# A mixture-of-experts layer whose stored expert results are weighted before they leave the chip and added to the residual stream by indirect DMAs

## The chip, the cores and the metric

The program runs on one core of a Trainium2 chip, in one launch. The metric is the device time of an execution in microseconds. The engines that appear below are PE (TensorE: matmuls and transposes), DVE (VectorE), ACT (ScalarE), POOL (GpSimd, which also issues the indirect DMAs) and SP (which issues plain DMAs). Each runs its own queue of instructions in order; semaphores tie them together. Line numbers (L1252) are those of the kernel before, unless the changed kernel is named.

## The reference

Two layers over 256 latent and 256 context tokens of width 1024, four blocks of 128 tokens; layer 1 gives out the latent tokens alone, so its experts work on two blocks. What matters here is the second half of a layer and the begin of the next:

```python
        h = _ln(x) * (1 + sc2) + sh2
        x = _ln_affine(ALPHA * x + g2 * _hier_moe(h, w_rg[l], b_rg[l], w_re[l], b_re[l], w1[l], w3[l], w2[l]),
                       ln2_g[l], ln2_b[l])
        # and the same for the context with sh2c, sc2c, g2c
...
def _hier_moe(h, w_rg, b_rg, w_re, b_re, w1, w3, w2):
    # top-1 group of 4, top-2 of its 8 experts: combine[t, e] holds the two weights of token t
    for e in range(N_EXPERTS):
        hidden = jax.nn.silu(h @ w1[e]) * (h @ w3[e])
        out = out + combine[..., e:e + 1] * (hidden @ w2[e])
```

`sh2`, `sc2`, `g2` come from `silu(c) @ w_mod[l] + b_mod[l]`, one set for latent tokens and one for context tokens. The next layer begins with `_ln(x) * (1 + sc1) + sh1` and the projection `h @ w_in[l]`.

## The kernel before

Every tile of size lies in units of 8 KB per partition that `Mem` hands out. Weights are a list in the order of use (`stream`); `pump` issues as many loads from it as units and a cap (`cap`, set per place from HC and MC) allow, and `drop` frees a unit when its matmuls are done. Expert weights are loaded by indirect DMAs that POOL issues (L142), all other weights by SP (L161). The modulation `c @ w_mod` is cut into steps of one 1 MB load and four matmuls (L320); those of the next layer are `fillers`, put by `fill(n)` where TensorE would wait.

Layer 0's experts are worked off in passes (`todo`, from PLAN). A pass gathers its tokens by one-hot matmuls (L1191), computes both up projections (`up`, L1204), transposes the hidden rows (`mid`, L1238) and multiplies by `w2`. The last two passes (HOME = 2) weight their results and add them over a one-hot matmul on chip (`back` L1227, `down` L1262, `combine` L1284). The twelve passes before these ("away") write theirs unweighted to the DRAM buffer `ys`: `put` copies the two halves of a 128x1024 tile out of PSUM, one on ACT and one on DVE (L1252), and SP stores it (L1254). Afterwards each token needs two rows of `ys`, its two experts: `fetch` gathers them by indirect DMAs into `ACC` and `two` (L1482), and `fold` does the rest for a block: ACT scales the first row by its weight (L1489), DVE adds the second times its weight (L1491), multiplies by g2 (L1492) and adds to `X` (L1493). Blocks 0 and 1 are fetched during the last two passes, blocks 2 and 3 behind the loop `rest`.

`rest` is a hardware loop over token lists that did not fit the plan; it runs no round in the profiled execution, but all engines pass its entry and exit (L1501), and nothing is moved across it. Behind it come the last `combine`, the second DeepNorm (`deepnorm`, `moments`: sums on DVE L427, means L414/L415, squares on ACT L416, inverse root on POOL L419, L431/L433 on DVE), the LayerNorm of the next layer, its transposes (`turned`, L489, evicted by ACT L497 and DVE L494), and the projection `p_qa`, three matmuls per product of split operands (L457 to L459). Before, loads for layer 1 are taken from the stream during the last expert passes, as units come free. A scheduler lays out each engine's queue from the order written here and priorities; `tc.issue_after` gives it an order.

## Time and profile before

| | us |
|---|---|
| median of 3 runs | 1111.08 (1108.67 to 1111.8) |
| profiled execution | 1106.13 |
| its span | 1104.2 |
| TensorE busy | 994.6 (90%) |
| DVE, ACT, POOL busy | 511.2, 353.1, 302.0 |
| layer 0's expert passes, by TensorE | 342.95 to 597.2 |
| layer 1's first projection begins | 642.61 |

Rows of a timeline give start, duration and instruction, and in brackets how long the engine stood idle before it and what ended that (`<-DMA u<-ys,find` is the landing of a DMA from `ys`). Rows of a group give the busy time in total and the mean of one in ns. Windows give per stretch the busy time of each engine, the granted clock of TensorE as a share of 2.4 GHz, the share of time in which the DMA engines moved data, and the rate.

### The profile page before, as it was taken

The page shows a single profiled execution, that of the slowest core. Times are in us where ns is not written, and L with a number is a line of the kernel's source. Part 1 is how long each engine was busy: PE and PEld are TensorE (multiplying, and loading weights), DVE is VectorE, ACT ScalarE, POOL GpSimd, SP SyncE. Part 2 cuts the span into 40 slices and gives each one's busy share as a digit, 9 for nine tenths or more (in the row PEclk, how much of TensorE's full clock was granted, in tenths as well). Part 3 has the DMA queues.
Part 4 walks back from the last instruction along what each step waited for, and adds up shares of the span by engine and source line. Part 5 has one row for each costly group of instructions (what it writes and reads, how often), then busy time and mean ns, then how long its engine had stood idle before and what let it go on. Part 6 is the DMA issues. An engine that isn't in the chain of part 4 may idle for free. (4 is left out here: it accounts for less than half of the span.)

```text
span 1104.2 us, 14811 instructions
## 1 busy us (share of the span) xinstructions
PE 994.6 (90%) x5525; PEld 571.6 (52%) x5525; DVE 511.2 (46%) x1364; ACT 353.1 (32%) x712; POOL 302.0 (27%) x325
## 2 busy tenths in 40 slices
PE   4999999999999999999985479999998899999894
PEld 2788745457866454444332259844466554433231
DVE  5643357775577210100013887266666654242244
ACT  4533155563552111111112365144444222111111
POOL 2111133350001432343341222042300145344420
PEclk9999999999999999999998789999997899999997
DMA  9812157610269999999998653435425799999992
GB/s 374 321 64 88 48 191 278 218 44 34 107 259 390 399 423 422 363 414 421 423 421 352 249 202 112 173 137 193 150 78 230 306 387 423 421 421 421 420 421 90
DMA packets 46207, 300.54 MB, mean 272 GB/s; under 512 B 5394, under 2 KB 5778, under 8 KB 14388
## 3 DMA queue, kind: packets, MB, share of 16 engines
q0 software_dynamic: 25824, 177.81, 39.2%
q1 hardware_dynamic: 20308, 121.75, 29.4%
q8 instruction: 45, 0.74, 0.3%
q14 instruction: 30, 0.25, 0.1%
HBM read 292.19 MB, written 7.34 MB: 271 GB/s over the span
## 5 line engine op out<-in xcount | busy, mean ns | idle before, releaser
L142 POOL DMA_INDIRECT u<-in_w_exp,u x162 | 161.1, 994 | 307.4 <-PE psa L1204 95.9
L1204 PE MATMUL psa<-u,u 128*32 128x512 f32 (+2 forms) x1040 | 212.9, 596 | 8.1 <-DMA u<-in_w_exp,u 8.1
L458 PE MATMUL psa<-u,u 128*128 128x512 f32 (+3 forms) x400 | 140.0, 351 | 2.2 <-DVE u L452 2.2
L457 PE MATMUL psa<-u,u 128*128 128x512 f32 (+3 forms) x400 | 140.8, 356 | 0.9 <-ACT u L506 0.7
L459 PE MATMUL psa<-u,u 128*128 128x512 f32 (+3 forms) x400 | 139.1, 351 | 0.1
L1204 PEld LDWEIGHTS psa<-u,u 128*32 128x32 f32 (+2 forms) x1040 | 64.6, 126 | 132.5 <-issue 109.1
L1191 PEld LDWEIGHTS psc<-u,u 128*128 128x128 f32 x640 | 83.0, 197 | 33.2 <-issue 29.0
L1191 PE MATMUL psc<-u,u 128*128 128x256 f32 x640 | 93.7, 297 | 3.0 <-DVE u L1177 2.1
L889 POOL TENSOR_SCALAR u<-u,ri 128x512 f32<-128x512 f32 (+1 forms) x48 | 68.4, 1430 | 99.1 <-DVE ri L887 81.5
L1211 DVE TENSOR_TENSOR scr<-scr,psa 128x256 f32<-128x256 f32 x26 | 10.9, 421 | 163.4 <-ACT scr L1210 157.7
L458 PEld LDWEIGHTS psa<-u,u 128*128 128x128 f32 x400 | 76.1, 190 | 12.9 <-DVE u L452 4.3
L457 PEld LDWEIGHTS psa<-u,u 128*128 128x128 f32 x400 | 75.5, 190 | 12.2 <-ACT u L506 1.1
L459 PEld LDWEIGHTS psa<-u,u 128*128 128x128 f32 x400 | 75.4, 190 | 9.3 <-issue 0.9
L886 ACT ACTIVATE u<-psa,nm 128x512 f32<-128x512 f32 (+1 forms) x96 | 58.4, 615 | 54.7 <-DVE nm L884 49.8
L1262 PE MATMUL pse<-u,scr 128*64 128x512 f32 (+1 forms) x288 | 70.4, 599 | 0.8 <-DMA u<-in_w_exp,u 0.8
L452 DVE TENSOR_TENSOR u<-u,u 128x1024 fp32r<-128x1024 f32 (+4 forms) x38 | 56.1, 1486 | 19.5 <-ACT u L451 19.4
L1210 ACT ACTIVATE scr<-psa 128x256 f32<-128x256 f32 x26 | 10.0, 385 | 171.5 <-PE psa L1204 171.5
L1193 ACT ACTIVATE u<-psc 128x512 f32<-128x512 f32 x52 | 31.1, 597 | 101.5 <-PE psc L1191 58.9
L884 DVE TENSOR_REDUCE nm<-psa 128x1 f32<-128x512 f32 (+1 forms) x80 | 53.1, 683 | 13.1 <-PE psa L874 9.5
L419 POOL TENSOR_TENSOR lns<-lns,mhalf 128x1 f32<-128x1 f32 x22 | 14.2, 648 | 162.7 <-DVE lns L418 130.3
L1249 PE MATMUL pse<-u,scr 128*32 128x512 f32 (+2 forms) x232 | 57.3, 600 | 1.4 <-ACT scr L1239 1.4
L451 ACT ACTIVATE u<-u 128x1024 fp32r<-128x1024 f32 (+4 forms) x38 | 47.4, 1266 | 16.2 <-PE psa L458 3.5
(317 smaller groups left out, 1366.5 us busy)
## 6 DMA issues: line engine op xcount, KB each, us to landing
u<-in_w_mod SPq DMA_DIRECT2D x48, 1024.0 KB, 6.5
u<-in_w_exp SPq DMA_DIRECT2D x30, 1024.0 KB, 6.9
u<-in_w_out SPq DMA_DIRECT2D x8, 1024.0 KB, 4.8
ys<-u SPq DMA_DIRECT2D x12, 512.0 KB, 8.2
u<-in_w_in_b SPq DMA_DIRECT2D x10, 512.0 KB, 11.7
u<-in_w_in_v SPq DMA_DIRECT2D x4, 960.0 KB, 5.9
u<-in_w_in_qa SPq DMA_DIRECT2D x4, 768.0 KB, 11.7
u<-in_ln_rows SPq DMA_DIRECT2D x6, 512.0 KB, 7.1
```

What stands on the lines that cost most here:

```text
L142: G.indirect_dma_start(out=b.ap(UNIT), out_offset=None, in_=wexp_rows, in_offset=bass.IndirectOffsetOnAxis(ap=idx, axis=0), bounds_check=N ...
L452: V.tensor_tensor(l_[:, c], w[:, c], h[:, c].bitcast(F32), OP.subtract)
L457: PE.matmul(p, lhsT=a[0], rhs=b[0], start=first, stop=False)
L458: PE.matmul(p, lhsT=a[0], rhs=b[1], start=False, stop=False)
L459: PE.matmul(p, lhsT=a[1], rhs=b[0], start=False, stop=final)
L884: V.tensor_reduce(out=nm[:, s, 0:n], in_=pv, axis=AX.X, op=OP.max, negate=True)
L886: S.activation(P[:, i, :], pv[:, i, :], AF.Exp, bias=nm[:, s, i:i + 1], accum_out=su[:, s, i:i + 1])
L889: (G if s == 0 else V).tensor_scalar(P[:, i, :], P[:, i, :], ri[:, s, i:i + 1], None, op0=OP.mult)
L1191: PE.matmul(pv[:, j, :], lhsT=H[b][:, k * 128:(k + 1) * 128], rhs=OH[:, b, :], start=(b == 0 and i == 0), stop=(b == nb - 1 and i == 1))
L1204: PE.matmul(g[r, :], lhsT=XG[:, k, at * 128 + r.start:at * 128 + r.stop], rhs=W(t, k // 4).v(4, 512)[:, k % 4, :], start=(k == 0), stop=(k ...
L1249: PE.matmul(y[r, :], lhsT=hc[:, c * 128 + r.start:c * 128 + r.stop], rhs=W(t, 2).v(2, D)[:, c, f * 512:f * 512 + 512], start=(c == 0), sto ...
L1262: PE.matmul(y[r, :], lhsT=hc[:, c * 128 + r.start:c * 128 + r.stop], rhs=W(t, 2).v(2, D)[:, c, f * 512:f * 512 + 512], start=(c == 0), sto ...
```

## The change

The weights and g2 are put on an expert's result before it is stored. `shares` forms, per away pass, two weights for each of the 128 rows, one if the row belongs to a latent token and one if to a context token (the other is zero), by four small matmuls; `put` computes y·w0·g2 + y·w1·g2c by two scalar_tensor_tensor on DVE and an add on POOL per half. `X` is scaled by ALPHA during pass 2, and `fetch` adds the rows of `ys` into `X` by an indirect DMA with `compute_op=add`, eight of them; `fold` and its buffers go, `yo` has two buffers for three, g2's rows are made at pass 0. Layer 1's part of the stream is held back until behind `rest` (`upto`; the first modulation group excepted), `rows()` (the DeepNorm's gain and bias, L1465) is loaded there too, and freshly freed units are used first for a while (`newest`). Its order mixes modulation steps between projections; of four `fill` steps ahead of the projections two go behind the two `p_b`. MC falls from 11 to 10 units and HC changes.

```diff
-MC = (11, 15)
+MC = (10, 15)
...
-HC = (8, 7, 3, 5)
+HC = (10, 10, 3, 3, 5)
...
@@ pump
+            if key[1] > upto[0] and key[0:3] != ("mod", 1, 0):
+                return
...
@@ the stream of layer 1
-    for k in ("qa", "cq"):
-        for c in range(2):
-            stream_chunk(k, 1, c)
+    for c in range(2):
+        stream_chunk("qa", 1, c)
+    stream_mod(1, 1, 0, 2)
+    for c in range(2):
+        stream_chunk("cq", 1, c)
     for c in range(2):
         stream_b(1, c)
-    stream_mod(1, 1, 0, 4)
+        stream_mod(1, 1, c + 2, c + 3)
...
@@ layer, its begin in layer 1
             rest_of()
+            fill(2)
             for c in range(2):
                 presplit("qa", c)
             make_h()
-            fill(4)
...
+            pump(HC[4])
+            mem.newest = False
             together(*[before(b, xn) for b in range(2, 4)])
             p_qa()
             p_cq()
             for c in range(2):
-                p_b(c)
+                gate[:] = [p_b(c)]
+                fill(1)
+            gate.clear()
...
+        def shares(q, at, n, m, col):
+            OH = ohs[q % len(ohs)].v(nb, 128 * n)
+            e = 128 // m
+            ws = sm.tile([128, 2], F32, name="ws", bufs=2)
+            p = bank("a")
+            for b in range(nb):
+                o = b // 2 * 2 * e
+                PE.matmul(p[:, o:o + 2 * e], lhsT=OH[:, b, at * 128:at * 128 + 128], rhs=IW[:, b, :, col:col + e],
+                          start=(b % 2 == 0), stop=(b % 2 == 1))
+            for t, r in enumerate(slots(m)):
+                V.tensor_reduce(out=ws[r], in_=p[r, 0:4 * e].rearrange("p (s i e) -> p s e i", s=2, i=2)[:, :, t],
+                                axis=AX.X, op=OP.add)
+            return ws
...
@@ put
-                d = Y[:, f * 512:f * 512 + 512]
-                V.tensor_copy(d, y) if f else S.activation(d, y, AF.Copy)
+                fs = slice(f * 512, f * 512 + 512)
+                w = scratch()
+                V.scalar_tensor_tensor(w, y, ws[:, 0:1], BC["g2", 0][:, fs], op0=OP.mult, op1=OP.mult)
+                V.scalar_tensor_tensor(Y[:, fs], y, ws[:, 1:2], BC["g2", 1][:, fs], op0=OP.mult, op1=OP.mult)
+                G.tensor_tensor(Y[:, fs], Y[:, fs], w, OP.add)
...
@@ fetch
-            for b in blocks:
-                acc[b] = mem.get(D)
-                ACC[b] = acc[b].v(D)
-                two.append(mem.get(D))
-                for dst, j in ((ACC[b], 0), (two[b].v(D), 1)):
-                    G.indirect_dma_start(out=dst, out_offset=None, in_=ys[:, :],
+            for j in range(2):
+                for b in blocks:
+                    G.indirect_dma_start(out=X[b], out_offset=None, in_=ys[:, :],
                                          in_offset=bass.IndirectOffsetOnAxis(ap=find[:, b, j:j + 1], axis=0),
-                                         bounds_check=at_row, oob_is_err=False)
+                                         bounds_check=at_row, oob_is_err=False, compute_op=OP.add)
-        def fold(blocks):
-            for b in blocks:
-                S.activation(ACC[b], ACC[b], AF.Copy, scale=sc_[:, b, 2:3])
-            for b in blocks:
-                V.scalar_tensor_tensor(ACC[b], two[b].v(D), sc_[:, b, 3:4], ACC[b], op0=OP.mult, op1=OP.add)
-                V.tensor_tensor(ACC[b], ACC[b], BC["g2", b // 2], OP.mult)
-                V.tensor_tensor(X[b], X[b], ACC[b], OP.add)
-                two[b].free()
...
@@ the passes, and behind them
+            if i < away:
+                ws = shares(q, at_, n, m, col)
             hc = mid(hb)
...
-                put(i, hc, m, W, rel)
+                put(i, hc, ws, m, W, rel)
...
         rest(slot[held[0]], qe % 2)
...
-        pump()
+        if not last:
+            mem.newest = True
+            rows()
+            upto[0] = 1
+            pump(HC[2])
...
-            fold(range(2))
```

The scheduler's order shows three places. On TensorE, in the changed kernel, the end of the fifth pass: `shares` is L1257, `mid`'s transposes are L1268, the last up matmuls L1219.

```order
L1219 MATMUL psa<-u_3732,u_3032 128x512 x4
L1257 MATMUL psa<-u_3036,u_3035 128x2 x4
L1268 MATMUL psa<-ident,scr 128x128 x2
L1219 MATMUL psa<-u_3728,u_3032 128x512
L1279 MATMUL pse<-u_3752,scr 128x512 x4
```

The four matmuls are new there; in the order before, the transposes follow the up matmuls directly.

On POOL, behind the loop `rest`, in the kernel before: L1482 are the fetches, L308 the loads of b_mod, L419 the inverse roots.

```order
L1482 DMA u_4690<-ys,find 128x1024
L1482 DMA u_5038<-ys,find 128x1024
L1482 DMA u_4697<-ys,find 128x1024 [waits DVE_49]
L308 DMA u_99<-in_b_mod 4x512 x2
L306 MEMSET u_99 128x512
L308 DMA u_99<-in_b_mod 4x512 [waits Pool_49]
L308 DMA u_99<-in_b_mod 4x512
L419 TENSOR_TENSOR lns<-lns,mhalf 128x1 [waits DVE_49] x6
```

And in the changed kernel, the same place, where L1508 are the adding fetches into `X` of blocks 2 and 3 (`u_72`), L315 the loads of b_mod, L427 the inverse roots.

```order
L1508 DMA u_72<-ys,find 128x1024 x2
L315 DMA u_99<-in_b_mod 4x512
L1508 DMA u_72<-ys,find 128x1024 [waits DMASW4_49]
L1508 DMA u_72<-ys,find 128x1024 [waits DMASW5_49]
L315 DMA u_99<-in_b_mod 4x512
L313 MEMSET u_99 128x512
L315 DMA u_99<-in_b_mod 4x512 [waits Pool_49]
L315 DMA u_99<-in_b_mod 4x512
L427 TENSOR_TENSOR lns<-lns,mhalf 128x1 [waits DVE_49] x6
```

The second add of each block now waits on POOL for a DMA, ahead of the inverse roots; before, no fetch behind the loop waits for another.

On DVE, before the evictions of the transposes (L494), in the kernel before: L1491 to L1493 are the fold of blocks 2 and 3, L1293 the evictions of `combine`.

```order
L437 TENSOR_TENSOR lns<-lns 128x1
L1491 SCALAR_TENSOR_TENSOR u_4697<-u_4998,sc__2337,u_4697 128x1024
L1491 SCALAR_TENSOR_TENSOR u_4690<-u_5038,sc__2337,u_4690 128x1024
L1492 TENSOR_TENSOR u_4697<-u_4697,u_4597 128x1024
L1492 TENSOR_TENSOR u_4690<-u_4690,u_4597 128x1024
L1493 TENSOR_TENSOR u_72<-u_72,u_4697 128x1024
L1493 TENSOR_TENSOR u_72<-u_72,u_4690 128x1024
L1293 TENSOR_TENSOR u_4697<-psa,u_4597 128x512 x2
L1293 TENSOR_TENSOR u_4690<-psa,u_4597 128x512 x2
L494 TENSOR_SCALAR scr<-psc,modT_100 128x256 x2
```

And in the changed kernel, where L443 is the former L437, L458 splits qa's weights, L433 adds `combine`'s rows to `X` of block 2, and L500 is the former L494.

```order
L443 TENSOR_TENSOR lns<-lns 128x1 [waits Pool_49]
L458 TENSOR_TENSOR u_5308<-u_5163,u_5307 128x512 [waits DMAHW1_49]
L458 TENSOR_TENSOR u_5308<-u_5163,u_5307 128x512 x2
L433 SCALAR_TENSOR_TENSOR u_72,dns<-u_72,u_5168 128x1024 [waits DMASW7_49]
L500 TENSOR_SCALAR scr<-psc,modT_100 128x256 [waits Activation_49] x2
```

The fold is gone from between the second norm's statistics and the evictions, and a sum that waits for the second adding fetch of block 2 stands in its place.

## Rows read from the trace of the kernel before

**Rows 1.** The page, busy time, share of the span and instructions of TensorE

```profile
PE 994.6 (90%) x5525; PEld 571.6 (52%) x5525; DVE 511.2 (46%) x1364; ACT 353.1 (32%) x712; POOL 302.0 (27%) x325
```

**Rows 2.** Windows around the seam: engines' busy us, clock, DMA share, GB/s

```profile
342.95:597.20 254.25, 239.13 (x1241) 108.00 (x1240) 36.72 (x121) 37.96 (x72) 88.25 (x89) 1.00 1.00 408
597.20:604.20 7.00, 0.02 (x1) 0.00 (x0) 3.08 (x3) 1.90 (x3) 0.00 (x0) 0.77 0.60 238
604.20:622.00 17.80, 12.51 (x48) 7.38 (x48) 14.45 (x28) 8.09 (x13) 7.75 (x10) 0.88 0.90 326
622.00:642.60 20.60, 6.80 (x32) 3.03 (x33) 18.59 (x37) 7.81 (x11) 2.32 (x3) 0.52 0.38 119
```

**Rows 3.** TensorE's timeline behind the loop: start us, us, instruction [idle before]

```profile
612.91 1.06 PE L320 MATMUL pse<-u,csil 128*32 128x512 f32 x8
...
629.52 1.54 PE L489 MATMUL psc<-ident,u 128*128 128x128 f32 x6 [1.40 <-ACT u L438]
638.03 3.64 PE L320 MATMUL pse<-u,csil 128*32 128x512 f32 x16 [6.97 <-DMA u<-in_w_mod]
...
642.61 0.42 PE L457 MATMUL psa<-u,u 128*128 128x384 f32 x1
```

**Rows 4.** TensorE's waits in the passes: us in total, times, longest

```profile
PE psa L1204 <- DMA u<-in_w_exp,u: 7.0, 5, 2.7
PE psa L1238 <- DVE scr L1211: 5.9, 6, 1.0
```

**Rows 5.** TensorE's timeline at the end of the passes

```profile
585.61 3.65 PE L1204 MATMUL psa<-u,u 128*64 128x512 f32 x14 [2.70 <-DMA u<-in_w_exp,u]
...
593.58 3.65 PE L1262 MATMUL pse<-u,scr 128*64 128x512 f32 x12 [0.21 <-DMA u<-in_w_exp,u]
604.47 6.39 PE L1284 MATMUL psa<-u,u 128*128 128x512 f32 x20 [7.25 <-issue]
```

**Rows 6.** Groups of the passes: busy us, mean ns, idle before

```profile
L1252 DVE COPY u<-pse 128x512 f32<-128x512 f32 x12 | 8.3, 691 | 67.1 <-PE pse L1249 67.1
...
L1227 PE MATMUL psa<-u,u 128*128 128x4 f32 x8 | 1.2, 256 | 0.0
```

**Rows 7.** SP's DMA issues for layer 1, first and last of seven

```profile
566.32 0.33 SPq L161 DMA_DIRECT2D u<-in_w_in_qa  x1
...
589.35 0.37 SPq L161 DMA_DIRECT2D u<-in_w_in_b  x1
```

**Rows 8.** Groups of the whole span

```profile
L889 POOL TENSOR_SCALAR u<-u,ri 128x512 f32<-128x512 f32 x32 | 51.4, 1608 | 65.0 <-DVE ri L887 65.0
...
L1271 DVE SCALAR_TENSOR_TENSOR u<-pse,ws,u 128x512 fp32r<-128x512 f32 x4 | 3.0, 749 | 8.7 <-ACT u L1270 8.7
```

**Rows 9.** DMA issues: count, KB each, median us to landing

```profile
ys<-u SPq DMA_DIRECT2D x12, 512.0 KB, 8.2
...
u<-in_w_exp,u POOLq DMA_INDIRECT x162, 16.4
```

**Rows 10.** SP's waits from 560 to 645: us in total, times, longest

```profile
SPq L1501 <- DMA u<-ys,find: 13.1, 4, 6.1
```

**Rows 11.** DVE's timeline around the end of the loop

```profile
599.98 0.74 DVE L1271 SCALAR_TENSOR_TENSOR u<-pse,ws,u 128x512 fp32r<-128x512 f32 x1
...
628.04 2.48 DVE L1491 SCALAR_TENSOR_TENSOR u<-u,sc__2337,u 128x1024 f32<-128x1024 f32 x2
...
634.97 2.48 DVE L1293 TENSOR_TENSOR u<-psa,u 128x512 f32<-128x512 f32 x4
637.37 0.99 DVE L494 TENSOR_SCALAR scr<-psc,modT 128x256 f32<-128x256 f32 x2
```

**Rows 12.** ACT's timeline behind the loop

```profile
612.96 1.15 ACT L1489 ACTIVATE u<-u,sc__2337 128x1024 f32<-128x1024 f32 x1 [5.39 <-DMA u<-ys,find]
```

**Rows 13.** POOL's timeline behind the loop

```profile
604.87 1.55 POOL L1482 DMA_INDIRECT u<-ys,find  x1 [14.35 <-issue]
...
618.18 0.94 POOL L419 TENSOR_TENSOR lns<-lns,mhalf 128x1 f32<-128x1 f32 x1 [5.69 <-DVE lns L418]
```

More of the change, by code (lines that the diff above doesn't have):

```diff
@@ L1 @@
 import math
-from contextlib import ExitStack
+from contextlib import ExitStack, nullcontext
 import numpy as np
@@ L135, in backbone @@
     ahead = [0]
+    upto = [0]
     cap = [6]
@@ L318, in step @@
             w = take(("mod", l, g, j)).v(4, 512)
-            for i in range(4):
-                PE.matmul(p[32 * i:32 * i + 32, :], lhsT=csil[:, j, :], rhs=w[:, i, :], start=(j == 0), stop=(j == 7))
+            with tc.issue_after(gate[0]) if gate else nullcontext():
+                for i in range(4):
+                    PE.matmul(p[32 * i:32 * i + 32, :], lhsT=csil[:, j, :], rhs=w[:, i, :], start=(j == 0), stop=(j == 7))
             drop(("mod", l, g, j))
@@ L1547, in layer @@
                 combine([(i - 1) % 2])
-            if i == away and away:
+            if i == 0 and away:
+                rows_g2()
+            if i == 2 and away:
                 for b in range(nb):
                     S.activation(X[b], X[b], AF.Copy, scale=ALPHA)
-            if i == end and away:
-                rows()
             if i == 1:
@@ L1592, in rest_of @@
             if not last:
-                with tc.issue_after(normed[-1]):
-                    fold(range(2, nb))
                 combine(fin, range(2, nb), True)
```

34 lines of the change are left out of this document (20 added, 14 removed).

## The prediction

> **What bounds the kernel now.** I read the page's busy times first, then the windows of the stretch that the change touches, then the waits of TensorE inside it, then the timelines of the engines around the end of layer 0's expert loop, because that is where the edits lie.
>
> The page has TensorE busy for 90% of the span [rows 1], so a microsecond counts only where TensorE works or is waited for. The windows divide the stretch [rows 2]. From 342.95 to 597.20 (twelve passes whose results go to DRAM and two that stay on the chip) TensorE is busy 239 of 254 us and the DMA engines are busy all the time, at 408 GB/s: both are close to the limit. From 597.20 to 604.20 TensorE does nothing, and from 604.20 to 642.60 it is busy 19.3 of 38.4 us, most of that at a reduced clock (0.88, then 0.52). So there are two places: a loop that TensorE and DMA bound together, and a seam of 45 us, until layer 1's first projection starts at 642.61 [rows 3], where chains on DVE, ACT, POOL and DMA decide.
>
> Inside the loop TensorE waits 7.0 us for expert weights, five times, 2.7 us of it at 585.61, and 5.9 us at the transposes L1238, six times, for DVE's L1211 [rows 4, 5].
>
> **The loop.** *Added on TensorE:* `shares`, four matmuls per away pass. The nearest row is L1227, the same four matmuls of the home passes: eight of them 1.2 us, with their overlap 0.54 us for four [rows 6]. Twelve passes make 6.5 us. In the order of the changed kernel they stand right in front of the transposes, and in four of the away passes that is where TensorE now waits about 1 us for L1211 (5.9 us over six, two of them home passes [rows 4]), so those four cost nothing: 8 x 0.54 = 4.3 us. If none is hidden it is 6.5; if the waits simply move, also 6.5.
>
> *Removed ahead of the weights:* before, seven loads for layer 1 (3.1 MB of projection weights, 1 MB of norm rows) are issued by SP between 566.32 and 589.35 [rows 7], into the DMA queues behind which the last experts land (TensorE's last wait for them ends at 593.58) [rows 5]. The first four of them (qa, two norm rows, qa), 2.6 MB, go out before that landing; at the loop's 408 GB/s [rows 2] they are 6.2 us. With the gate `upto` they stand behind the loop. The weights then come up to 6 us earlier than now, and TensorE's last two waits (2.7 and 0.2 us) go, with a third of 1.35 us among the five of rows 4: 4.3 us, at most all 7.2. So the loop ends at 597.2 + 4.3 - 4.3, that is unchanged, with 594.3 (all waits gone) and 599.5 (no share hidden, half of the waits left) as its ends.
>
> *put:* the ACT copy and the DVE copy of 128x512 per pass (0.69 us on DVE [rows 6]) become four scalar_tensor_tensor of 0.75 us on DVE and two adds on POOL (DVE's L1271; for POOL's two-input add there is no 128x512 row, the nearest is the one-input L889 of 1.6 us [rows 8]). DVE has 36.7 us of work in 254, ACT 38, POOL 88 [rows 2], so 12 x 2.3 us on DVE and 12 x 3.2 us on POOL fit beside. What is queued behind the POOL adds counts, though: POOL issues the expert loads in order, and an add that waits for DVE holds the loads behind it by some 2 to 3 us per pass.
>
> POOL is idle 166 us of the loop now, waiting for slots; from issue to landing an expert load takes 16.4 us [rows 9], so a hold of 3 us is covered while that backlog lasts. I take 0, with 3 us as the far end. MC 10 for 11 I cost at nothing: the loads that are out before the loop are bounded by memory, not by this cap; if that is wrong it is one expert unit of 1 MB, 2.5 us of DMA, covered by a prefetch that is landed before the first pass. g2's rows move from pass 12 to pass 0, the same instructions.
>
> **Leaving the loop.** `rest` runs no round, but every engine passes its gate, and SP there waits for the DMAs that are out: 13.1 us in four waits on the fetches `u<-ys,find` [rows 10]. The last five loads of layer 1 and the fetches of blocks 0 and 1 are what lands last, and DVE's last eviction of the pass runs at 599.98 because the fold stands ahead of it [rows 11]; TensorE continues at 604.47, 7.25 us after its last matmul [rows 5]. After: no layer-1 load but one w_mod step, four adding fetches of 0.5 MB; the first two can go when the last store has landed (about 577 by the stores' 8.2 us [rows 9]), the second of a block only when the first has landed. At the plain rate that is 1.25 us each and about 3 us of latency: done near 592. What ends last then is TensorE at 597.2 and its eviction, 0.75 us, and the barrier, for which no row stands and which I put at 0.9 us: 599.3. Gain 4.9 us; ends 2.0 (loop end 599.5 and a landing that is late by a little) and 7.5.
>
> **From the loop to the first projection, 38.4 us now** (604.2 to 642.61). Before, ACT stands 5.39 us at L1489 until a fetch lands at 612.96, so the first inverse root on POOL (L419) is at 618.18, 14.0 us after the loop [rows 12, 13]. Then 11.3 us to the second pair of transposes, 629.52 [rows 3]. Their evictions on DVE (L494) come only at 637.37, since the fold of blocks 2 and 3 and its evictions occupy DVE from 628.04 [rows 11]: 7.3 us that the transposed rows lie. From 637.37 to 642.61 it is 5.2 us, of which 3.64 us is four w_mod steps L320, which start at 638.03 after 6.97 us of waiting for their weights and stand ahead of the last transposes [rows 3]. Sum 14.0 + 11.3 + 7.9 + 5.2 = 38.4.
>
> After: no fold. DVE starts with some table products and memsets, then the evictions. But on POOL the first adds, b_mod and *the second adds of blocks 2 and 3* stand ahead of the first inverse root, and a second add waits for its first to land. In the trace of before a fetch issued at 604.87 is what ACT waits for until 612.96, 8.1 us, with 2 MB of w_mod queued ahead [rows 12, 13]. The queues hold about as much after (1 MB of norm rows, 1.5 MB of qa). So the second adds go out at 8 to 10 us and the first inverse root is at about 11.5 instead of 14.0. From there 11.3 us to the transposes as before. L494's successor waits behind one 1.2 us sum of block 2 instead of 9.3 us: 1.6 instead of 7.9. The last leg is 5.2 less the difference between four and one w_mod step, 2.7, plus late qa splits, which I take as 2: 4.5. Together 11.5 + 11.3 + 1.6 + 4.5 = 28.9, a gain of 9.5. Ends: 25 (POOL not held: first root at about 8) and 34 (qa or the adds 5 us later).
>
> Two of the four w_mod steps move behind `p_b`, onto a TensorE that is then busy: eight matmuls, 1.06 us [rows 3]. Loss 1.1.
>
> **Sum:** -4.9 - 9.5 + 1.1 = -13.3 us on the profiled execution of 1106.1, so 1092.8. The median shown is 5.0 us above that execution: 1097.8, **1098 us**. From the ends of the terms: -2.0 - 4.4 + 1.1 = -5.3 (1106) to -7.5 - 13.4 + 1.1 = -19.8 (1091).
>
> **Rivals.** *Slower: the adding DMA.* The trace of before has no DMA that adds. A plain fetch of 0.5 MB is 1.25 us of all queues at the loop's rate; adding may be no dearer, or several times. Let the factor be f. The four adds before the gate have from 577 to about 597: 6 + 4 x 1.25f fits up to f = 2.8. Behind the loop the root on POOL comes after two first adds, and DVE's sum of block 2, which stands ahead of the evictions for qa, after its second add. At f = 4: gate at 604, no gain; second adds issued at 17, landed at 30, projection at about 35: gain 3.5 - 1.1, so 1109. At f = 6: gate at 613 (9 lost), projection at 45 (7 lost): 1128. It decides from f = 4.5 on. For it: a block's two adds are in series, where now no fetch waits for another. Against: indirect transfers make up most of the loop's bytes and move at the full 408 GB/s, so POOL's queue is not what limits them. Cheaper than a plain fetch an add can't be, since the same rows move.
>
> *Half rate.* f = 2: the gate is not touched, the second adds go out some 3 us later, and block 2's sum 3 to 4 us later: 1102 to 1104. The Trainium skill, page "Collectives: The Full Stack", section "The bandwidth ceiling: the fold count and why AG ≠ RS ≠ AR", gives this as a rule for a DMA that adds: it needs two source reads, and so runs at half the rate of a copy, in that page for transfers between cores; no run here shows it yet.
>
> *The loads are only postponed.* The 4.2 MB held back are 10 us of DMA after the loop, in a stretch whose DMA share is 0.90 and then 0.38 [rows 2]: 8.2 MB move there now (17.8 us at 326 GB/s and 20.6 at 119), 12.4 after, against 11.8 in 29 us at the loop's 408 GB/s. If qa's four splits or cq come 6 to 10 us late, the gain of the seam is gone and the kernel is at 1105 to 1111, no change. Against it: qa is second in the queue, and only qa is wanted by 29 us.
>
> *More gain.* If the first adds land in 5 us, POOL is free at 7 and the chain is 25 us, and the loop ends at 595: 1091.
>
> **Chances.** The forecast 0.42 (own range 1094 to 1103), more gain 0.13, half rate 0.17, postponed loads 0.12, slow adding DMA 0.16. The measurement of this kernel can tell about 0.3% from no change, 3.3 us. Half rate is nearly all faster (0.16 of 0.17), postponed loads are 0.03 faster, 0.06 the same, 0.03 slower, the slow adding DMA is 0.03 the same and 0.13 slower. Faster: 0.42 + 0.13 + 0.16 + 0.03 = 0.74; same: 0.01 + 0.06 + 0.03 = 0.10; slower: 0.03 + 0.13 = 0.16. Range 1088 to 1114.
>
> **What would show it.** Loop: L1204's waits for weights under 3 us and four of L1238's waits gone; TensorE's last matmul of it within 594 to 599. Gate: SP's waits there no longer on fetches, TensorE going on by 600. Seam: no L1489, L1491 to L1493; the POOL rows in order add, add, b_mod, add, add, root, the root 11 to 12 us after the gate; qa's matmuls 27 to 31 us after. It is wrong if an adding fetch takes more than about 5 us by itself on a free queue, if TensorE waits for weights in the loop longer than before (POOL's adds holding the loads), or if cq and b keep TensorE waiting after qa.

## The result and the profile after

The median goes from 1110.76 us to 1123.59 us (1119.90 to 1128.77 over four runs): a ratio of 1.0121, with an interval of 1.0078 to 1.0164. The kernel is slower by 13 us, 1.2%, where 13 us less were forecast. The profiled execution takes 1123.93 us, its span is 1122.2. The two profiled executions lie 17.8 us apart, the medians 12.8, so some 5 us of what the legs below add up to are the spread between executions.

I cut the traces at the same points: TensorE's first up matmul of layer 0's passes, its last one there, its first instruction behind the loop, and its first matmul of layer 1's projection, attention and routing. The third column is a second look at the kernel before (experiment 5).

| leg, us | before | before again | after |
|---|---|---|---|
| up to the passes | 342.9 | 344.7 | 344.9 |
| the passes | 254.3 | 254.0 | 258.1 |
| last matmul to TensorE going on | 7.3 | 7.4 | 11.5 |
| from there to the first projection | 38.1 | 37.9 | 36.2 |
| first projection to attention | 89.2 | 89.8 | 93.5 |
| attention to routing | 107.9 | 109.4 | 113.3 |
| the rest | 264.5 | (lengthened) | 264.7 |

The first leg varies by 2 us without the change, so it isn't the change's. The others lose 3.8 to 5.4 us each in four places and win 1.9 us in the one from which 9.5 were expected. The leg from attention to routing is 1.5 us longer in the second look as well, so of its 5.4 us 3.9 are left.

TensorE's waits in the passes, after (us in total, times, longest):

```profile
PE psa L1268 <- DVE scr L1226: 7.6, 8, 1.0
PE psc L1206 <- DVE u L1192: 4.9, 4, 1.8
PE pse L1279 <- ACT scr L1269: 2.5, 5, 0.5
PE psa L1219 <- DMA u<-in_w_exp,u: 1.4, 1, 1.4
```

The waits for weights fall from 7.0 to 1.4 us [rows 4], as forecast; experiment 3 puts the reason in doubt. But the transposes wait eight times instead of six, and there is a wait that was not there: for the one-hot tiles L1192 of the next gather, which DVE makes.

The groups that the change puts into the passes (busy us, mean ns, idle before):

```profile
L1285 POOL TENSOR_TENSOR u<-u,scr 128x512 f32<-128x512 f32 x24 | 30.7, 1280 | 62.1 <-DVE u L1284 61.8
L1283 DVE SCALAR_TENSOR_TENSOR scr<-pse,ws,u 128x512 f32<-128x512 f32 x24 | 18.0, 748 | 56.1 <-PE pse L1279 52.8 <-issue 3.3
L1284 DVE SCALAR_TENSOR_TENSOR u<-pse,ws,u 128x512 f32<-128x512 f32 x24 | 17.8, 742 | 0.0
```

POOL's add is 1.28 us, less than the bound of 1.6 [rows 8]; it stands 62 us idle in its queue until DVE's product is there, and what is queued behind it stands with it.

TensorE around the end of the loop, after (start us, us, instruction, idle before):

```profile
599.33 3.70 PE L1295 MATMUL pse<-u,scr 128*64 128x512 f32 x16
614.50 10.07 PE L1317 MATMUL psa<-u,u 128*128 128x512 f32 x32 [11.47 <-issue]
633.36 1.93 PE L328 MATMUL pse<-u,csil 128*32 128x512 f32 x8 [8.79 <-DMA u<-in_w_mod]
643.35 0.69 PE L495 MATMUL psc<-ident,u 128*128 128x128 f32 x2 [8.05 <-ACT u L444]
...
650.68 0.42 PE L463 MATMUL psa<-u,u 128*128 128x384 f32 x1
```

Against [rows 3, 5] the loop's end is at 603.0 instead of 597.2, the gate opens 11.5 instead of 7.3 us later, and the first projection is at 650.7. Before, the combine was mixed with sixteen modulation matmuls; here it stands alone. It runs at a reduced clock, as its first twenty matmuls did before (6.39 us for twenty [rows 5], here 10.07 for thirty-two).

The windows, after (engines' busy us, granted clock, DMA share, GB/s), answer to [rows 2]:

```profile
344.92:603.10 258.18, 240.37 (x1289) 116.49 (x1288) 65.43 (x178) 29.94 (x60) 118.99 (x111) 0.99 0.97 390
603.10:614.50 11.40, 0.00 (x0) 0.00 (x0) 1.48 (x4) 0.65 (x1) 1.59 (x2) 0.64 0.66 121
614.50:632.00 17.50, 10.07 (x32) 7.78 (x32) 8.38 (x38) 5.19 (x9) 6.72 (x6) 0.70 0.97 297
632.00:650.70 18.70, 7.59 (x33) 3.47 (x33) 14.36 (x33) 9.16 (x13) 5.14 (x9) 0.50 0.71 208
```

In the second window the engines hardly work and the DMA engines move 121 GB/s while their share is 0.66: what is out there is slow for its bytes. TensorE's clock is 0.70 and then 0.50 (1.2 GHz) where it was 0.88 and 0.52.

POOL from the last expert load on, after; L1508 are the adding fetches, L427 the first inverse root:

```profile
588.95 0.98 POOL L145 DMA_INDIRECT u<-in_w_exp,u  x1 [5.13 <-DMA ys<-u]
590.23 1.59 POOL L1508 DMA_INDIRECT u<-ys,find  x1 [0.30 <-issue]
592.13 1.58 POOL L1508 DMA_INDIRECT u<-ys,find  x1 [0.30 <-issue]
601.59 1.55 POOL L1508 DMA_INDIRECT u<-ys,find  x1 [7.88 <-DMA u<-ys,find]
606.44 1.55 POOL L1508 DMA_INDIRECT u<-ys,find  x1 [3.29 <-DVEq L1517]
614.93 1.56 POOL L1508 DMA_INDIRECT u<-ys,find  x1 [6.95 <-issue]
616.79 1.55 POOL L1508 DMA_INDIRECT u<-ys,find  x1 [0.30 <-issue]
...
625.75 1.64 POOL L1508 DMA_INDIRECT u<-ys,find  x1 [6.73 <-DMA u<-ys,find]
630.70 1.56 POOL L1508 DMA_INDIRECT u<-ys,find  x1 [3.31 <-DMA u<-ys,find]
...
634.84 0.59 POOL L427 TENSOR_TENSOR lns<-lns,mhalf 128x1 f32<-128x1 f32 x1
```

This queue tells much of the story. The last expert load waits 5.1 us for a store of `ys`, since its unit was `yo`'s; the fetches stand behind it and start at 590, not at 577. Of blocks 0 and 1 the first adds land 11.1 and 13.6 us after their issue, the second ones go out at 601.6 and 606.4, when the first have landed, and land at 609.3 and 613.3; the gate opens 1.2 us after the last landing. Behind the gate the same happens again with blocks 2 and 3, and the first root waits behind it: 20.3 us after the gate, where it was 13.7 [rows 13]. DVE shows what that costs:

```profile
623.93 0.15 DVE L426 TENSOR_SCALAR lns<-lns 128x1 f32<-128x1 f32 x1
...
624.60 0.14 DVE L422 TENSOR_SCALAR lns<-dns 128x1 f32<-128x1 f32 x1
624.66 0.14 DVE L423 TENSOR_SCALAR lns<-dns 128x1 f32<-128x1 f32 x1
635.47 1.28 DVE L439 SCALAR_TENSOR_TENSOR u<-u,lns,u 128x1024 f32<-128x1024 f32 x1 [10.67 <-POOL lns L427]
```

DVE has the statistics ready for the root with L426, at 624.1, and stands 10.67 us for a root of 0.6 us.

### The profile page after: what moved, and what is told of

It is laid out like the page before. It is cut to its first block, busy times and chain, and to the rows that moved or that the text cites. A ratio compares the mean times of both kernels' runs of the same rounds, so it can differ in the third digit from the quotient of the medians.

```text
span 1122.2 us, 14967 instructions
## 1 busy us (share of the span) xinstructions
PE 1001.2 (89%) x5573; PEld 586.4 (52%) x5573; DVE 528.2 (47%) x1417; ACT 342.1 (30%) x696; POOL 336.9 (30%) x349
## 3 DMA queue, kind: packets, MB, share of 16 engines
q1 hardware_dynamic: 20308, 121.75, 28.9%
## 5 line engine op out<-in xcount | busy, mean ns | idle before, releaser
L1219 PE MATMUL psa<-u,u 128*32 128x512 f32 (+2 forms) x1040 | 214.8, 596 | 2.5 <-DMA u<-in_w_exp,u 2.5
L464 PE MATMUL psa<-u,u 128*128 128x512 f32 (+3 forms) x400 | 142.5, 357 | 4.5 <-DVE u L458 4.5
L463 PE MATMUL psa<-u,u 128*128 128x512 f32 (+3 forms) x400 | 143.7, 363 | 2.6 <-ACT u L457 1.7
L465 PE MATMUL psa<-u,u 128*128 128x512 f32 (+3 forms) x400 | 141.1, 356 | 0.1
L1219 PEld LDWEIGHTS psa<-u,u 128*32 128x32 f32 (+2 forms) x1040 | 66.1, 126 | 122.4 <-issue 106.5
L1206 PEld LDWEIGHTS psc<-u,u 128*128 128x128 f32 x640 | 85.3, 202 | 35.1 <-issue 26.3
L463 PEld LDWEIGHTS psa<-u,u 128*128 128x128 f32 x400 | 77.7, 195 | 15.5 <-ACT u L457 2.5
L464 PEld LDWEIGHTS psa<-u,u 128*128 128x128 f32 x400 | 78.1, 195 | 14.8 <-DVE u L458 6.0
L465 PEld LDWEIGHTS psa<-u,u 128*128 128x128 f32 x400 | 77.5, 195 | 8.7 <-DVE u L513 0.3
L458 DVE TENSOR_TENSOR u<-u,u 128x1024 fp32r<-128x1024 f32 (+4 forms) x38 | 56.1, 1486 | 28.3 <-ACT u L457 25.3
L1295 PE MATMUL pse<-u,scr 128*64 128x512 f32 (+1 forms) x288 | 67.3, 599 | 0.6 <-DMA u<-in_w_exp,u 0.6
L427 POOL TENSOR_TENSOR lns<-lns,mhalf 128x1 f32<-128x1 f32 x22 | 13.5, 615 | 152.8 <-DVE lns L426 122.4
L1317 PE MATMUL psa<-u,u 128*128 128x512 f32 x128 | 40.4, 446 | 15.5 <-issue 11.5
```

The costliest lines, as they stand in the source:

```text
L458: V.tensor_tensor(l_[:, c], w[:, c], h[:, c].bitcast(F32), OP.subtract)
L463: PE.matmul(p, lhsT=a[0], rhs=b[0], start=first, stop=False)
L464: PE.matmul(p, lhsT=a[0], rhs=b[1], start=False, stop=False)
L465: return PE.matmul(p, lhsT=a[1], rhs=b[0], start=False, stop=final).ins
L1206: PE.matmul(pv[:, j, :], lhsT=H[b][:, k * 128:(k + 1) * 128], rhs=OH[:, b, :], start=(b == 0 and i == 0), stop=(b == nb - 1 and i == 1))
L1219: PE.matmul(g[r, :], lhsT=XG[:, k, at * 128 + r.start:at * 128 + r.stop], rhs=W(t, k // 4).v(4, 512)[:, k % 4, :], start=(k == 0), stop=(k ...
```

## The experiments

Twelve kernels ran. Theory A at the begin: the adding DMA is slow, so that the gate and POOL's queue wait for it. Rivals: it moves at half rate only and what costs is the order in series; the postponed loads cost; the passes cost. Each column is one profiled execution. The passes are the same code in the changed kernel and in experiments 1, 2, 6, 7 and 9, and take 258.1 to 261.0 us there, so differences of up to 3 us in that row say nothing.

| leg, us | e1 | e2 | e3 | e4 | e6 | e7 | e8 | e9 | e10 | e11 | e12 |
|---|---|---|---|---|---|---|---|---|---|---|---|
| passes | 258.9 | 260.6 | 254.5 | 270.3 | 258.1 | 259.8 | 251.3 | 261.0 | 261.9 | 252.8 | 253.4 |
| to the gate's opening | 6.4 | 11.0 | 10.8 | 12.5 | 2.2 | 11.4 | 11.6 | 5.7 | 4.8 | 6.0 | 7.7 |
| opening to first root | 17.0 | 9.6 | 20.7 | 20.5 | 12.1 | 19.9 | 20.3 | 10.8 | 10.5 | 13.8 | 13.4 |
| opening to projection | 32.2 | 28.9 | 35.3 | 33.7 | 29.9 | 34.6 | 35.8 | 27.2 | 27.0 | 29.8 | 27.4 |
| projection to attention | 93.3 | 93.2 | 93.1 | 89.1 | 99.0 | 88.7 | 93.5 | 97.3 | 98.1 | 94.4 | 97.4 |
| attention to routing | 110.9 | 111.2 | 110.7 | 112.4 | 110.8 | 112.3 | 113.4 | 112.2 | 112.2 | 108.0 | 110.0 |

**1. Plain gathers in place of the adding ones.**

```diff
-    bounds_check=at_row, oob_is_err=False, compute_op=OP.add)
+    bounds_check=at_row, oob_is_err=False)
```

> The changed kernel, with the eight fetches as plain gathers into X (the addition is left out, so X holds only the second row; layer 1's routing then differs, and times are read only up to layer 1's first projection). Theory A, the add itself is slow: on a queue with nothing else a fetch lands about 3 us after its issue instead of 6.9 to 7.7, the loop's gate lets TensorE go on at 605 to 607 instead of 614.5, POOL's first inverse root comes 14 to 16 us behind the gate instead of 20.3, and the first projection at 632 to 637 instead of 650.7. Rival B, the order in series alone: landing times and gate stay within 1 us of the changed kernel's.

The gate opens at 610.4, the root comes 17.0 us behind it, the first projection at 642.6. Each is between the two expectations: the add itself costs 5 us at the gate and 4 behind it, about half of what theory A wanted. The order in series is still there; experiment 6 takes it away. (Layer 1's lists of tokens differ here, so its 1156 us say nothing.)

**2. The second adds of blocks 2 and 3 behind the roots.**

```diff
-            fetch(range(2, nb))
+            fetch(range(2, nb), (0,))
...
+                with tc.issue_after(roots[-1]):
+                    fetch(range(2, nb), (1,))
```

> The changed kernel, with the second adds of blocks 2 and 3 put behind the four inverse roots of blocks 0 and 1 on POOL. Theory, POOL's queue is held: gate as before the edit (614 to 615), the first root 10 to 11 us behind the gate instead of 20.3, the first projection at 640 to 643 instead of 650.7, the whole 7 to 10 us below the changed kernel. Rival, the chain is bound by late loads (qa lands at 629.3, a w_mod step at 633.3): first projection no earlier than 647, whole time within 4 us of the changed kernel's.

1115.83 us, 7.8 below the changed kernel (1.0069 of before, 1.0039 to 1.0100). POOL's queue now:

```profile
617.57 1.56 POOL L1510 DMA_INDIRECT u<-ys,find  x1 [6.46 <-issue]
619.43 1.55 POOL L1510 DMA_INDIRECT u<-ys,find  x1 [0.30 <-issue]
...
626.73 0.58 POOL L429 TENSOR_TENSOR lns<-lns,mhalf 128x1 f32<-128x1 f32 x1 [2.58 <-DVE lns L428]
...
639.75 2.21 POOL L1510 DMA_INDIRECT u<-ys,find  x1 [0.18 <-issue]
642.26 1.91 POOL L1510 DMA_INDIRECT u<-ys,find  x1 [0.30 <-issue]
```

The root waits for DVE again and not for a landing, and the leg is 28.9 us. The hold of POOL's queue is shown, with 7.3 us. The gate opens as late as in the changed kernel (11.0 us after the last matmul). The first projection is at 646.1, between the two expectations, since the passes end 3.1 us later in this execution.

**3. The passes with the old put, without shares.**

```diff
-                w = scratch()
-                V.scalar_tensor_tensor(w, y, ws[:, 0:1], BC["g2", 0][:, fs], op0=OP.mult, op1=OP.mult)
-                V.scalar_tensor_tensor(Y[:, fs], y, ws[:, 1:2], BC["g2", 1][:, fs], op0=OP.mult, op1=OP.mult)
-                G.tensor_tensor(Y[:, fs], Y[:, fs], w, OP.add)
+                d = Y[:, fs]
+                V.tensor_copy(d, y) if f else S.activation(d, y, AF.Copy)
...
-                ws = shares(q, at_, n, m, col)
+                ws = None
```

> The changed kernel with the loop's old put (one copy on ACT, one on DVE, no shares; the rows are stored unweighted, so the result lacks weights and g2 on them). Theory: shares and POOL's adds in front of the expert loads cost the loop about 4 us, and the store of the last away pass goes out some 3 us earlier: TensorE's last matmul of the loop at 598 to 600 instead of 603.0, the gate 4 to 6 us earlier. Rival, the loop's loss comes from g2's rows at pass 0 and from the caps: last matmul still at 602 or later.

The passes take 254.5 us, as before, with the last matmul at 600.1, and the gate opens at 610.9, 3.6 us earlier. What lengthens the passes is shares and put together, not g2's rows or the caps. But TensorE waits for weights as long as in the kernel before, though layer 1's loads are held back here too:

```profile
PE psa L1219 <- DMA u<-in_w_exp,u: 6.6, 6, 2.1
```

So that holding them back takes these waits away is not shown; longer passes also leave the weights more time.

**4. Layer 1's loads not held back.**

```diff
-HC = (10, 10, 3, 3, 5)
+HC = (8, 7, 3, 3, 5)
...
-    upto = [0]
+    upto = [1]
...
-            mem.newest = True
             rows()
```

> The changed kernel with layer 1's loads not held back and the caps 8 and 7 as in the kernel before (two norm rows, two qa, two w_mod steps go out ahead of the loop's gate again). Theory: the postponed loads are not what costs; qa then lands before the root, yet the first projection moves by less than 3 us from 650.7 and the gate comes 3 to 6 us later, since the adds queue behind 4 MB; whole time within 4 us of the changed kernel's. Rival, the postponed loads cost the seam: gate as now, first projection at 640 to 645, whole time 6 to 10 us below.

Both were wrong. The leg to attention falls from 93.5 to 89.1 us, which is before's: that loss comes with the postponed loads (experiment 7 says by what). But the passes take 270.3 us and the whole 1130.32. TensorE waits 5.3 us for weights, 2.7 at once; that is 3.9 more than in the changed kernel, but less than the 7.0 of the kernel before [rows 4]. For the rest it is busy longer with the same matmuls, 248.8 us instead of 240.4, in part at a reduced clock behind the late waits (0.89 from 600 to 616 us; the last sixteen take 5.39 us, where they take 3.70 in the changed kernel). In this kernel the postponement is needed; why the kernel before bears these loads among its passes is open.

**5. The adding DMA by itself.** The kernel before, and behind its last result:

```diff
+    for i in range(4):
+        pull(i)
+    for i in range(4):
+        pull(i, compute_op=OP.add)
+    for i in range(3):
+        pull(0)
+    for i in range(3):
+        pull(0, compute_op=OP.add)
```

> The kernel before, with fourteen indirect DMAs of the fetch's shape (128 rows of 4 KB) put behind its last result, when no other transfer is out: four plain ones into four tiles, four adding ones into the same tiles, three plain ones and three adding ones in series into one tile. Theory: an adding one in series takes 6.5 to 7.5 us from issue to landing and a plain one 2.5 to 3.5; four adding ones side by side are at least 3 us apart, four plain ones 1.2 to 1.4. Rival (half rate): the adding ones are 2.5 us apart and 4 to 5 us in series. The rest of the trace is a second look at the kernel before: layer 0's passes end 254 to 255 us after they begin, and from attention to layer 1's routing it takes 108 us if that leg's 113 in the changed kernel is the change's, up to 111 if such a leg also varies without it.

POOL's timeline of the last five, two plain and three adding ones in series:

```profile
1124.74 1.00 POOL L1623 DMA_INDIRECT u<-in_x,row  x1 [7.68 <-DMA u<-in_x,row]
1129.22 0.99 POOL L1623 DMA_INDIRECT u<-in_x,row  x1 [3.49 <-DMA u<-in_x,row]
1133.72 1.56 POOL L1623 DMA_INDIRECT u<-in_x,row  x1 [3.50 <-DMA u<-in_x,row]
1140.14 1.56 POOL L1623 DMA_INDIRECT u<-in_x,row  x1 [4.86 <-DMA u<-in_x,row]
1146.90 1.55 POOL L1623 DMA_INDIRECT u<-in_x,row  x1 [5.20 <-DMA u<-in_x,row]
```

A plain one needs 4.2 us from issue to landing (1124.74 to 1128.97, 1129.22 to 1133.46), an adding one 6.0 to 6.5 (1133.72 to 1139.88, 1140.14 to 1146.64, 1146.90 to 1152.87), and POOL is busy 1.56 us with its issue instead of 1.0. Side by side, the four adding ones land at 1115.78, 1118.24, 1120.71 and 1123.20: 2.47 us apart, 0.5 MB each, 212 GB/s. That is half of the 408 GB/s of the passes [rows 2], and half of what plain gathers reach in experiment 6, where four land 1.25 us apart (596.54 to 600.29); the four plain ones of this run are 1.8 us apart. Theory A's 3 us apart do not come: the adding DMA runs at half rate, as the rival had it. By itself it takes longer than the rival's 4 to 5 us, and a plain one longer than the theory's 2.5 to 3.5.

The Trainium skill, page "Collectives: The Full Stack", section "The bandwidth ceiling: the fold count and why AG ≠ RS ≠ AR", puts a transfer that adds at half the rate of a copy because of its two source reads; for a gather from DRAM into the chip this run agrees with the half, 212 against 408 GB/s. No run here tests that reason.

**6. Blocks 0 and 1 by plain gathers and DVE adds, beside the late adds of blocks 2 and 3.**

```diff
+                    if b < 2:
+                        got[b, j] = mem.get(D)
...
+        def fold():
+            for b in range(2):
+                for j in range(2):
+                    V.tensor_tensor(X[b], X[b], got[b, j].v(D), OP.add)
```

> The changed kernel with the second adds of blocks 2 and 3 behind the roots, and with blocks 0 and 1 fetched by plain gathers into tiles of their own, which DVE adds into X behind the loop. Theory: no two slow adds in series in front of the gate, so TensorE goes on 6 to 7 us behind its last matmul instead of 11, the root 12 to 14 us behind that (four DVE adds of 1.2 us), the whole 1110 to 1113, that is about the kernel before. Rival, the gate is not what the adds cost: within 2 us of the run with late adds alone (1115.8).

1109.90 us, 0.2% above the kernel before (1.0023, 1.0005 to 1.0041). The gate opens 2.2 us after the last matmul instead of 11.0, and the first projection is at 632.0, 10.6 us earlier than in the kernel before. With experiment 1, where the gate opened 6.4 us after the last matmul, this gives the order in series 4.2 us at the gate. Nearly all of the 10.6 us is given back in the next leg, 99.0 us against 89.2. Part of it is the late adds; a row of DVE's timeline and one of TensorE's waits:

```profile
634.79 1.23 DVE L435 SCALAR_TENSOR_TENSOR u<-u,u 128x1024 f32<-128x1024 f32 x1 [3.24 <-DMA u<-ys,find]
PE psa L467 <- DVE u L515: 3.5, 1, 3.5
```

DVE stands 3.24 us for the landing of block 2's second add, the split of the transposed rows (L515) stands behind that sum, and TensorE waits 3.5 us for it. It waits 3.2 us more for splits of weights (L460) and 2.9 for the rotated rows (L617).

**7. The old order of layer 1's loads.**

```diff
-    stream_mod(1, 1, 0, 2)
...
-        stream_mod(1, 1, c + 2, c + 3)
+    stream_mod(1, 1, 0, 4)
...
-            fill(2)
+            fill(4)
...
-                gate[:] = [p_b(c)]
-                fill(1)
+                p_b(c)
```

> The changed kernel with the kernel before's order of layer 1's loads (modulation steps behind the projections) and its four modulation steps in one place. Theory: the order of the stream does not cost; what is postponed does: from the first projection to attention 92 to 95 us (changed kernel 93.5, before 89.2), the whole within 4 us of the changed kernel's. Rival, the mixed order costs it: 89 to 90 us for that leg.

The leg to attention is 88.7 us, so the rival is right: the loads of experiment 4 cost that leg only in the mixed order. Two `w_in_b` loads land at 610.3 and 613.1 here (issued at 599.4 and 605.4, ahead of the loop), at 653.1 and 654.3 in the changed kernel. The whole is 1117.61, 6.0 below the changed kernel.

**8. Shares with the old copies.** As experiment 3, with shares kept: the last edit of its diff is undone.

```diff
-                ws = None
+                ws = shares(q, at_, n, m, col)
```

> The changed kernel with shares computed but the old copies in put (rows are stored unweighted). Theory: the four matmuls of shares cost TensorE 3 to 4 us over the passes, with the copies' loop at 254.5 us, so the passes take 257 to 259 us as in the changed kernel, and DVE's two products and POOL's add cost the loop next to nothing. Rival, POOL's adds hold the expert loads and DVE's products the one-hot tiles: passes 254 to 256 us, and the difference to 258 is theirs.

The passes take 251.3 us, 6.8 less than in the changed kernel: the rival's side, and less than it said. Shares cost nothing that can be seen; put's products do. The one-hot wait is down to

```profile
PE psc L1206 <- DVE u L1192: 1.8, 4, 0.7
```

from 4.9 us. That is 3.1 of the 6.8; the waits for weights give another 1.4, and TensorE is busy 2.1 us less with the same matmuls, for which no run gives the reason. That POOL's adds hold the expert loads, the other half of that rival, is not yet apart from DVE's load; experiment 10 does that.

This run also tells of the gate. Its first adds go out where the prediction had them, at 579.5 (it said 577), and not at 590:

```profile
579.45 1.59 POOL L1506 DMA_INDIRECT u<-ys,find  x1 [0.30 <-issue]
581.35 1.58 POOL L1506 DMA_INDIRECT u<-ys,find  x1 [0.30 <-issue]
591.93 1.55 POOL L1506 DMA_INDIRECT u<-ys,find  x1 [9.00 <-DMA u<-ys,find]
597.41 1.55 POOL L1506 DMA_INDIRECT u<-ys,find  x1 [3.93 <-DMA u<-ys,find]
```

Still the gate opens 11.6 us after the last matmul (11.5 in the changed kernel), and in experiment 3, where they go out at 579.0, 10.8 us after it. Among the loop's last loads the first two need 12.2 and 15.3 us to land, the second two 7.3 and 6.8, and all is in at 604.2.

**9. Experiments 6 and 7 together**, both diffs as they stand there.

> The run with plain gathers for blocks 0 and 1 and late adds for blocks 2 and 3, and beside that the kernel before's order of layer 1's loads and its four modulation steps in one place. Theory: that run won 10 us up to the first projection and gave back 10 us up to attention (99.0 us for that leg, where the old order took 88.7 in the changed kernel), so the leg falls to 89 to 92, the first projection comes 1 to 3 us later for the four steps, and the whole is 1100 to 1104, faster than the kernel before. Rival: the postponed loads take what the seam gains whatever their order, the leg stays at 95 or more and the whole at 1107 to 1111.

1109.58 us (1.0004, 0.9989 to 1.0018): the rival. The first projection comes 27.2 us behind the gate, but the leg to attention stays at 97.3 us. Two of TensorE's waits and one of SP's, from the last matmul to attention:

```profile
PE pse L326 <- DMA u<-in_w_mod: 14.7, 2, 12.1
PE psa L1316 <- DMA u<-in_w_in_b: 5.7, 1, 5.7
SPq L1527 <- DMA u<-in_w_in_b: 3.6, 1, 3.6
```

The 5.7 us are the gate itself. The fetches are in at 603.8, but a load of `w_in_b`, which the program asks for only behind `rest`, is issued at 603.44 ahead of it, and SP waits for it there; in experiments 7 and 10 to 12 such loads go out ahead of it as well. So that nothing is moved across the loop does not hold for these loads, and the gate, 2.2 us in experiment 6, is 5.7 here.

Added up, the two legs from the gate to attention are 127.4 us in the kernel before and 129.7 in the changed one; 122.1, 122.7, 123.2 and 124.4 us in experiments 2, 4, 7 and 9. With the gate, that is from the last matmul of the passes to attention, they are 134.6 before and 141.2 in the changed kernel, 133.1, 134.6 and 131.2 in experiments 2, 7 and 6, and 130.1 here. Together the edits so win 11.0 us, more than each, and stand 4.5 us below the kernel before. The whole is no faster since the passes (261.0 against 254.3) and the leg from attention to routing (112.2 against 107.9) lose more than that. The rival's number came, and not by the postponed loads alone. Which load or which unit holds the leg to attention at 97.3 us I have not settled.

**10. Put's sum on DVE instead of POOL**, on experiment 9.

```diff
-                G.tensor_tensor(Y[:, fs], Y[:, fs], w, OP.add)
+                V.tensor_tensor(Y[:, fs], Y[:, fs], w, OP.add)
```

> The same, with the sum of the two weighted halves in put on DVE (12 x 2 x 0.69 us) instead of POOL. Theory that POOL's adds hold the expert loads: the passes take 252 to 255 us instead of 258, the whole 3 to 5 us below the run with POOL's adds. Rival, it is DVE's share of put that delays the one-hot tiles (4.9 us of waits at the gather): with 16.6 us more on DVE the passes take 259 to 262 us, the whole 1 to 4 us above it.

The passes take 261.9 us, the whole 1111.01 (1.0025, 1.0007 to 1.0042), 0.9 and 1.4 more than experiment 9: the rival's numbers, though a difference of this size is not clear of the spread. What is clear is that the passes get no shorter without POOL's adds. The one-hot wait grows, experiment 9 above, this one below:

```profile
PE psc L1205 <- DVE u L1191: 4.4, 4, 1.8
PE psc L1205 <- DVE u L1191: 7.3, 2, 3.8
```

So with experiment 8 it is DVE's work in put that lengthens the passes, in part by way of the one-hot tiles queued behind it, and not POOL's adds ahead of the loads.

**11. Only the token's weight before the store, g2 behind the fetch**, on experiment 9.

```diff
-                V.scalar_tensor_tensor(w, y, ws[:, 0:1], BC["g2", 0][:, fs], op0=OP.mult, op1=OP.mult)
-                V.scalar_tensor_tensor(Y[:, fs], y, ws[:, 1:2], BC["g2", 1][:, fs], op0=OP.mult, op1=OP.mult)
-                G.tensor_tensor(Y[:, fs], Y[:, fs], w, OP.add)
+                if f:
+                    V.tensor_scalar(Y[:, fs], y, one_w, None, op0=OP.mult)
+                else:
+                    S.activation(Y[:, fs], y, AF.Copy, scale=one_w)
...
+                V.tensor_tensor(A, A, BC["g2", b // 2], OP.mult)
+                V.tensor_tensor(X[b], X[b], A, OP.add)
```

Blocks 2 and 3 gather their first row into a tile `A`, add the second to it by DMA, and go through the last two lines behind the first transposes.

> The run with plain gathers, late adds and the old order of loads, with only the token's weight put on a row before it is stored (the copies on ACT and DVE take it as their scale); g2 is multiplied in behind the fetches by DVE, for blocks 2 and 3 behind the first transposes. Theory, DVE's four products per pass are what lengthens the passes: they take 252 to 255 us instead of 261, the two more DVE operations per block cost the seam 2 to 3 us, and the whole is 1103 to 1107, a little faster than the kernel before. Rival: the passes' loss is the transposes' waits behind DVE's L1211 (eight of them, 7.6 us) and shares, which stay: 258 us or more, the whole no better than 1109.

1102.84 us, 0.9948 of the kernel before (0.9929 to 0.9967): 0.5% faster than the kernel before. The passes take 252.8 us; of the waits on one-hot tiles 1.8 us are left:

```profile
PE psa L1269 <- DVE scr L1227: 6.6, 7, 1.0
PE pse L1282 <- ACT scr L1270: 2.6, 5, 0.5
PE psc L1207 <- DVE u L1193: 1.8, 3, 0.8
```

The transposes' waits and shares are still in it, so they are not what cost.

**12. One more unit for the loads behind the loop**, on experiment 11.

```diff
-HC = (10, 10, 3, 3, 5)
+HC = (10, 10, 4, 4, 6)
```

> The same with one more unit for layer 1's loads at each place behind the loop (caps 4, 4, 6 instead of 3, 3, 5). Theory: the leg from the first projection to attention is bound by loads that wait for units behind the loop, so it falls from some 97 us by 3 to 6 and the whole by as much. Rival: it is bound by the DMA rate itself, since 4 MB more have to come in after the loop, or by TensorE's modulation steps: less than 2 us.

1106.01 us, 3 more than without. The leg to attention is 97.4 us and not shorter. It has 42 modulation matmuls in it now and had 34, and none stand between the gate and the projection any more; the two legs together take 124.8 us against 124.2. More units for loads are not what they lack.

## Why the prediction was wrong

*The bound was read rightly, the places too.* Passes, gate and seam are among the places where the time moved. Two legs behind them moved as well, and of those one was costed at nothing and the other not looked at.

*The loop, "unchanged", end 594.3 to 599.5:* it ends at 603.0, 258.1 us after its begin, 3.8 more (2.0 us of the later end were there before it). The waits for weights fell as forecast, but experiment 3 has them at 6.6 us with the same loads held back, so the reason given is not shown. The step that failed is "12 x 2.3 us on DVE ... fit beside": by busy share they do, but without the products the passes are 6.8 us shorter (experiment 8), and with a single scaling in their place 252.8 us (experiment 11). The one-hot tiles of the next gather stand behind the products in DVE's queue, which is 3.1 of the 6.8. That shares would hide in the transposes' waits was wrong as well, since those waits went from six to eight; with the old copies shares cost nothing all the same. (The end 599.5 should be 600.1: 597.2 and 6.5, less half of 7.2.) The hold of POOL's loads, which I had named as the risk, was not the cause (experiment 10).

*The gate, 599.3, gain 4.9:* 614.5, a loss of 10.0, of which 5.8 are the later end of the passes. The step that failed is "1.25 us each and about 3 us of latency: done near 592". The chain itself (two adds, then two that wait for them) is right, but no row gave the 3 us. By itself an adding fetch takes 6.0 to 6.5 us, a plain one 4.2 (experiment 5), and among the loop's last loads the first two take 11 to 15; the prediction had 16.4 us for an expert load [rows 9] and did not use it for the fetches. In the kernel before, fetches issued from 571 to 579 landed 23 to 25 us later. "About 577" for the start failed as well: the last store goes out at 580.11, POOL waits for it with the last expert load until 588.95, and the first add goes out at 590.2. But that is not what opens the gate late: in experiments 3 and 8 the adds start at 579, and the gate still opens 10.8 and 11.6 us after the last matmul. The barrier's 0.9 us, for which no row stood either, are small beside this: the gate opens 1.2 us after the last landing. (597.2, 0.75 and 0.9 add up to 598.9, not to 599.3.)

*The seam, gain 9.5:* 1.9. The step that failed is "the second adds go out at 8 to 10 us and the first inverse root is at about 11.5": they go out at 11.2 and 16.2 and the root is at 20.3. The hold of POOL's queue was seen and priced at a third, 3.5 us (11.5 against 8) where it is 10.7 (20.3 against 9.6 in experiment 2). With the second adds behind the roots the leg is 28.9 us, the sum of the forecast; that is in part luck, since there the root comes at 9.6 instead of 11.5 us and the way from it to the projection takes 19.3 instead of 17.4.

*The modulation steps, loss 1.1:* the trace before has 32 of their matmuls between gate and projection, sixteen mixed with the combine and sixteen at 638.03, and the changed kernel 16. The other sixteen went into attention (96 there instead of 80), twice the number that was priced. (The seam's last leg took off three steps, 2.7 us, where the change moves two, 1.8.) At 1.06 us for eight [rows 3] that is 2.1 of the 3.9 to 5.4 us of that leg. Over all the runs the leg goes with their number: 107.9 to 109.4 us with 78 or 80 of them (both looks at the kernel before, experiment 11), 110.0 with 86 (experiment 12), 110.7 to 113.4 with 96 (the others). No run changes that number alone, so this is not shown as the cause.

*The projections, costed at nothing:* 4.3 us. The rival "the loads are only postponed" was right in part: held back and in the mixed order they cost this leg, in the old order they don't in experiment 7, where two of them go out ahead of the loop all the same; not held back they don't either (experiment 4). Experiment 9, in the old order too, has 97.3 us for the leg, so the order is not the whole of it. It was wrong in where: it looked for the loss ahead of the first projection.

*The rivals:* the adding DMA at half rate is what the chip does, and with it alone I had expected 1102 to 1104. The slow adding DMA, which stood for slower, did not happen. The slower result came of the order in series and of queues, which I had put into that rival only as an aggravation. Of the signs of being wrong one came: an adding fetch takes more than 5 us by itself.

## What to carry to other kernels

An engine with free time still delays what stands behind new work in its queue: look for the next instruction on that engine that another one waits for, and not at the busy share. Two DMAs that must follow each other cost two whole latencies on the engine that issues them, and everything queued behind; put what is short and wanted ahead of the second. Take the latency of a DMA from rows of the place where it will run, with the loads that are out there, and not from its bytes. A load that is moved out of a busy stretch is still to be made: follow it to the stretch in which it then lands.

## What the runs showed of the hardware

An adding gather of 128 rows of 4 KB occupies POOL for 1.55 to 1.59 us to issue in experiment 5, a plain one for 1.0 to 1.1. It moves 212 GB/s side by side with others of its kind, half of the 408 GB/s of the loop's loads, and takes 6.0 to 6.5 us by itself, where a plain one takes 4.2; among the loop's last loads it took 11.1 to 15.3 us. The hardware loop that runs no round still waits for the DMAs that are out, fetches, expert loads or a load of `w_in_b`: TensorE goes on 2.2 to 12.5 us after its last matmul, by what lands last, and 1.2 to 1.4 us after the last fetch has landed in the kernel before, the changed one and experiment 8.
